# One more gate projection by seven products, and its gate written over a buffer that is already there

## The chip, the cores and the metric

The kernel runs on one core of one Trainium2 chip. The metric is the device time of one execution in microseconds (us). The kernel before takes 1662.96 us, the median of three runs that lie between 1662.33 and 1663.71 us.

A core has engines that run side by side, each with its own list of instructions in a fixed order. TensorE (PE in the profile, PEld for its weight loads) multiplies matrices. VectorE (DVE) and ScalarE (ACT) work elementwise. GpSimd (POOL) here issues most transfers and reduces a column over all partitions. SyncE (SP) issues the other transfers. On-chip memory (SBUF) has 128 partitions, and products accumulate in a second memory (PSUM).

## The reference

Two layers. Each normalises its input `h` (512 tokens of 2048 values), projects it, runs three groups of heads side by side, multiplies each by its own SiLU gate, and projects the result into the residual stream. What matters here is the short convolution, since the change lies in its gate, and the gated linear attention (GLA), whose work lies beside it:

```python
proj = h @ w_in
u = c_gate * h                                   # cv_c * cv_h
y = conv3(u) ; y_conv = cv_b * (y + bias) * silu(cv_g)
q, k, v, g = ...                                 # GLA: chunks of 64 tokens, state carried along
y_gla = rmsnorm(gla(q, k, v, g)) * silu(gl_g)
y_sb  = stick_breaking(...) * silu(sb_g)
out   = x + concat(y_conv, y_sb, y_gla) @ w_out
```

Each branch of the convolution (`h`, `b`, `c`, `g`) is 512 columns wide.

## The kernel before

**Weights.** All weight matrices are cut into groups of 256 columns (`specs`), taken one after the other. In each layer these are GLA's v 0, v 1, q, k, gate 0 and gate 1, then conv h 0, c 0, g 0 and b 0 (the first half of the convolution), then v, g, q and k for each of four pairs of attention heads, then conv h 1, c 1, g 1 and b 1, then eight groups of the output projection. A group of 2048x256 fp32 comes from DRAM into one of two buffers named `st`, as two transfers (`fetch`, L355, on POOL's queue). The transfer of group i+2 is issued when the computation of group i begins, and it has to wait until the last instruction has read the buffer that it goes to, so for the splits of group i (which shares the buffer).

**Splits.** Products are computed in fp16 with operands split into a high and a low part, three products for each. The scale of a group comes from squares of all its values (`wmax`, ACT at L367, twice, into an accumulator), a reduction over the partitions (POOL at L381) and four tiny instructions on DVE (L384 to L399). Then ACT writes the high part and DVE the low part. A plain group does so in two halves of 128x2048 (`whi` L436 and `wlo` L443). These steps of group i+1 hang on matmuls of group i (`hook`).

**Plain and quick groups.** A plain group of this kind is 96 matmuls of 128x512 (`project_cols`, L673 to L675). A group named in `QUICK_IN` is computed by seven products of half-size blocks in place of eight (`project_quick`, L765): 168 matmuls of 128x256. For this, `wsums` forms sums of the four weight blocks: one by an accumulating transfer within the buffer (L504, on POOL's queue), three by DVE (L507, L509, L512), and it splits seven parts of 128x1024 (ACT at L486, DVE at L487). The seven results are combined into the output by three copies on ACT (L780, L784, L787) and five instructions on DVE (L781, L788, L789, L791, L793). The blocks' sums for the input (`insums`) are made once in a layer. PSUM has three banks for projections.

**The convolution.** `conv_in(0)` projects h into `hb` (a buffer with the tag `qT`), then c, and multiplies the two into `uc` (L1167). After that nothing reads `hb`. `conv_out(0)` projects the gate with `project_gate`: for a plain group the gate is scaled out of PSUM into a buffer with the tag `g` (L842), and SiLU follows in steps (L844 to L848). Then it projects b, multiplies, and splits the result for the output projection with `mixsplit`, which uses the gate's buffer, dead by then, as its room.

**GLA.** It runs in two halves of two heads, interleaved with the groups on each engine. The decays of a chunk are made on DVE (L1038 to L1047) and ACT (L1002, L1011, L1040), put together on DVE (L1003, L1012), multiplied on PE (L1017, and then L1112), and closed by a norm (L1118 to L1130: PE averages at L1120, ACT and DVE finish).

**Order.** After a hand-ordered start, a scheduler in the compiler sets the fixed order of each engine, working with its own estimate of when each instruction could run. The code's `high_priority` blocks pull fetches, squares and splits ahead. A change in the code so moves other instructions too. The order of both kernels is known before they run; what it costs is not.

Of the kernel before, what the change touches and what calls it, by code (L numbers as in the profile page):

```python
# [17 lines left out]
P = 128  # L18
# [9 lines left out]


QUICK = ((3, 4, 6), (3, 4, 5, 6))  # L30
QUICK_IN = ("conv c 1", "gla gate 1", "conv g 1") + tuple(f"{n} {j}" for n in "gqk" for j in range(4))

AHEAD = (8, 17, 21)

# [9 lines left out]
def hybrid_trunk(ctx, tc, x, norm_g, w_in, conv_w, conv_b, sb_qn_g, sb_kn_g,  # L44
# [4 lines left out]
    seq = x.shape[1]  # L49
# [607 lines left out]
    for l in range(depth):  # L657
# [161 lines left out]
                ps.append(o)  # L819
                yield t, o, u  # L820

        def project_gate(mx=None, logistic=False):

            g = []

            def dst():
                g.append(wk([P, 2, seq], "g"))
                return g[0]

            ps, u = project(True, dst)  # L830
            quick_ = bool(g)
            g = dst() if not quick_ else g[0]
            for c in range(2):
                y = g[:, c, :]
                if logistic:
                    a = wk([P, seq], "ga") if quick_ else y
                    tables.append(S.activation(a, ps[c], AF.Sigmoid, scale=u))
                    for b in tables[-9:-1]:
                        order(tables[-1], b)
                    V.scalar_tensor_tensor(y, ps[c], u, a, ALU.mult, ALU.mult)  # L840
                    continue
                S.activation(y, ps[c], AF.Copy, scale=u)  # L842
                a = wk([P, seq], "ga")
                S.activation(a, y, AF.Abs)  # L844
                S.activation(a, a, AF.Exp, scale=-1.0)
                S.activation(a, a, AF.Ln, bias=1.0)
                V.scalar_tensor_tensor(a, y, 0.0, a, ALU.min, ALU.subtract)
                tables.append(S.activation(a, a, AF.Exp))  # L848
                V.tensor_tensor(y, y, a, ALU.mult)
            if mx is not None:  # L850
                V.tensor_reduce(mx, g, AX.XY, ALU.max, apply_absolute_value=True)
            return g, u
# [114 lines left out]
        for tag in ("qT", "kT"):  # L967
            o = wk([P, 2, seq], tag)
            ps, u = project(True, lambda: o)
# [187 lines left out]
        def conv_in(j, then=lambda: None):  # L1157

            hb = wk([P, 2, seq], "qT")
            ps, u = project(True, lambda: hb)  # L1160
            for c in range(2):
                S.activation(hb[:, c, :], ps[c], AF.Copy, scale=u)
            then()
            uc = wk([P, 2, seq], "raw", 1) if j else wk([P, 2, seq], "zw")
            ps, u = project(True, lambda: uc)
            for c in range(2):
                V.scalar_tensor_tensor(uc[:, c, :], ps[c], u, hb[:, c, :], ALU.mult, ALU.mult)  # L1167
            if j:
                mixload()
            y = wk([P, 2, seq], "kT")  # L1170
            for c in range(2):
                ch = 2 * j + c

                def w_(i):
                    return pcol("cw", (l * 3 + i) * 4 + ch)

                V.tensor_scalar(y[:, c, :], uc[:, c, :], w_(2), pcol("cb", l * 4 + ch), ALU.mult, ALU.add)
                for d in (1, 2):
                    V.scalar_tensor_tensor(y[:, c, d:], uc[:, c, :seq - d], w_(2 - d), y[:, c, d:], ALU.mult, ALU.add)
            then()  # L1180
            return y

        def conv_out(j, y, then=lambda: None):

            g, u = project_gate(logistic=j == 1)
            V.tensor_tensor(y, y, g, ALU.mult)
            bound = sm(2, "cm")

# [15 lines left out]
            for c in range(2):  # L1204
                mixsplit(2 * j + c, y[:, c, :], s_, g[:, c, :])

        conv_out(0, conv_in(0, lambda: norms.pop(0)()))


        later = []  # L1210
# [136 lines left out]
                go()  # L1347
            attend(j, *qkT, qz, vh, vl, vu, g, s_)

        conv_out(1, conv_in(1, go), go)  # L1350
        while later:
            go()
        if not last:
# [83 lines left out]
```

## Time and profile before

| | us |
|---|---|
| median of three runs | 1662.96 |
| the profiled execution: its time | 1662.23 |
| the profiled execution: span in the trace | 1660.4 |
| PE busy | 1636.1 (99%) |
| DVE busy | 1403.3 (85%) |
| ACT busy | 1181.9 (71%) |
| POOL busy | 258.6 (16%) |

The granted TensorE clock is 0.999 over the span. A row of a timeline gives the start of an instruction, its duration, engine, line, operation, what it writes and reads, the shapes and how many stand together; in brackets it tells how long the engine had been idle before it, and what released it. A matmul's duration contains its way through the array, and the next one starts before it ends: the distance of two starts is what one costs. In the table of windows each engine's busy time stands with its count of instructions in the order PE, PEld, DVE, ACT, POOL, then the granted clock, the share of the transfer engines and GB/s.

### The profile page before, as it was taken

What the parts mean: (1) busy time and instruction counts of PE and PEld (TensorE: products, weight loads), DVE (VectorE), ACT (ScalarE), POOL (GpSimd) and SP (SyncE); (2) the same over time, 40 slices, a digit from 0 to 9 for tenths busy, and PEclk for the clock granted to TensorE, in tenths of its full rate; (3) what the DMA queues carried; (4) which work ended last, traced back from release to release, by engine and by line L of the source; (5) the groups of instructions that cost most, each with busy time, mean ns of one, the idle gap of its engine ahead of it and who ended that gap; (6) DMA issues with size and microseconds to landing.
All of it is one profiled execution on the core that took longest, in us unless ns stands there. A gap on an engine that the chain in (4) does not pass through costs nothing. (4 is left out here: it accounts for less than half of the span.)

```text
span 1660.4 us, 39947 instructions
## 1 busy us (share of the span) xinstructions
PE 1636.1 (99%) x17098; PEld 1324.7 (80%) x17098; DVE 1403.3 (85%) x2323; ACT 1181.9 (71%) x1739; POOL 258.6 (16%) x298
## 2 busy tenths in 40 slices
PE   7999999999999999999999999999999999999999
PEld 5746548999998967799986465589898989668998
DVE  8978789979898979897599696998898989788893
ACT  8668787877777776755675786888686868666571
POOL 1121012111212121011111110112121212111110
PEclk9999999999999999999999999999999999999999
DMA  7144324576776868456433433436677676783441
GB/s 260 52 153 114 102 65 86 134 151 147 161 152 155 159 153 202 155 166 206 161 102 102 114 111 100 121 83 168 123 164 149 146 163 141 158 238 128 153 154 52
DMA packets 189747, 232.71 MB, mean 140 GB/s; under 512 B 90162, under 2 KB 149884, under 8 KB 189056
## 3 DMA queue, kind: packets, MB, share of 16 engines
q0 software_dynamic: 72832, 175.12, 38.9%
q1 hardware_dynamic: 107728, 45.56, 13.5%
q10 hardware_dynamic: 9008, 9.45, 1.7%
q8 instruction: 134, 2.20, 0.5%
q14 instruction: 45, 0.37, 0.1%
HBM read 179.65 MB, written 14.68 MB: 117 GB/s over the span
## 5 line engine op out<-in xcount | busy, mean ns | idle before, releaser
L486 ACT ACTIVATE wh<-st,ws 128x1024 f16<-128x1024 f32 x222 | 248.5, 1146 | 171.3 <-DVE st L507 68.1
L487 DVE SCALAR_TENSOR_TENSOR wl<-st,ws,wh 128x1024 f16<-128x1024 f32 x222 | 279.6, 1279 | 26.8 <-ACT wh L486 26.5
L367 ACT ACTIVATE junk<-st 128x2048 uint8<-128x2048 f32 x150 | 285.4, 1902 | 20.9 <-DMA st<-in_w_in_dram 13.9
L443 DVE SCALAR_TENSOR_TENSOR wl<-st,ws,wh 128x2048 f16<-128x2048 f32 x78 | 182.7, 2347 | 28.9 <-ACT wh L436 28.5
L685 PE MATMUL psp<-wl,m 128*128 128x256 f16 x704 | 191.9, 273 | 0.0
L684 PE MATMUL psp<-wh,m 128*128 128x256 f16 x704 | 191.9, 273 | 0.0
L686 PE MATMUL psp<-wh,m 128*128 128x256 f16 x704 | 191.9, 273 | 0.0
L436 ACT ACTIVATE wh<-st,ws 128x2048 f16<-128x2048 f32 x76 | 150.9, 1996 | 52.5 <-DVE ws L397 26.4
L768 PE MATMUL psp<-wh,s 128*128 128x128 f16 x2048 | 178.2, 219 | 3.9 <-DVE raw L788 3.7
L768 PEld LDWEIGHTS <-s 128*128 128x128 f16 x3072 | 173.2, 98 | 5.0 <-issue 4.7
L768 PE MATMUL psp<-wl,s 128*128 128x128 f16 x1024 | 172.8, 219 | 0.0
L381 POOL PARTITION_ALL_REDUCE wgm<-wm x75 | 43.1, 575 | 751.6 <-ACT junk L367 736.8
L355 POOL DMA_DIRECT2D st<-in_w_in_dram x114 | 101.8, 898 | 322.8 <-DVE wl L443 166.4
L765 PE MATMUL psp<-s,wh 128*128 128x256 f16 x896 | 151.9, 273 | 0.0
L765 PEld LDWEIGHTS <-wh 128*128 128x128 f16 x1344 | 131.4, 98 | 16.1 <-issue 1.0
L768 PEld LDWEIGHTS <-m 128*128 128x128 f16 x2160 | 122.7, 98 | 1.4 <-issue 1.0
L765 PE MATMUL psp<-s,wl 128*128 128x256 f16 x448 | 122.0, 273 | 0.0
L675 PEld LDWEIGHTS <-wl 128*128 128x128 f16 x576 | 56.3, 98 | 67.5 <-DVE wl L443 1.6
L675 PE MATMUL psp<-x,wl 128*128 128x512 f16 x288 | 109.0, 379 | 0.4 <-DVE wl L443 0.4
L674 PE MATMUL psp<-m,wh 128*128 128x512 f16 x288 | 109.2, 379 | 0.0
L674 PE MATMUL psp<-x,wh 128*128 128x512 f16 x288 | 109.2, 379 | 0.0
L675 PE MATMUL psp<-m,wl 128*128 128x512 f16 x288 | 109.0, 379 | 0.0
(422 smaller groups left out, 4147.8 us busy)
## 6 DMA issues: line engine op xcount, KB each, us to landing
st<-in_w_in_dram POOLq DMA_DIRECT2D x114, 1024.0 KB, 8.3
st<-in_w_out_dram POOLq DMA_DIRECT2D x32, 1024.0 KB, 8.4
st<-st POOLq DMA_DIRECT2D x30, 512.0 KB, 7.6
st<-in_w_in_dram SPq DMA_DIRECT2D x6, 1024.0 KB, 11.7
mixd<-g POOLq DMA_DIRECT2D x24, 256.0 KB, 5.7
x<-in_x_dram SPq DMA_DIRECT2D x4, 1024.0 KB, 4.8
qT<-in_x_dram ACTq DMA_DIRECT2D x8, 512.0 KB, 4.1
qT<-xs ACTq DMA_DIRECT2D x8, 512.0 KB, 3.9
```

The costliest lines, as they stand in the source:

```text
L367: sq = S.activation(junk(HK * GW).rearrange("p (k n) -> p k n", k=HK), staged[i][h], AF.Square, accum_out=peak[i][:, h:h + 1])
L436: hi = S.activation(wh[:, :, :GW], staged[i][h], AF.Copy, scale=scales[i])
L443: V.scalar_tensor_tensor(wl[:, :, :GW], staged[i][h], scales[i], wh[:, :, :GW], ALU.mult, ALU.subtract)
L486: hi = S.activation(h_, b, AF.Copy, scale=sc)
L487: V.scalar_tensor_tensor(l_, b, sc, h_, ALU.mult, ALU.subtract)
L674: T.matmul(o, wh[:, kk, cs], xl[:, :, k, :], start=False, stop=False)
L675: mm = T.matmul(o, wl[:, kk, cs], xh[:, :, k, :], start=False, stop=en)
L684: T.matmul(o, ah[:, t, k, :], wh[:, kk, :n], start=st_, stop=False, skip_group_check=True)
L685: T.matmul(o, ah[:, t, k, :], wl[:, kk, :n], start=False, stop=False, skip_group_check=True)
L686: return T.matmul(o, al[:, t, k, :], wh[:, kk, :n], start=False, stop=en, skip_group_check=True)
L765: mm = T.matmul(o, w[q_][:, kk, :], a[p_][:, :, kk, :], start=st_, stop=en, skip_group_check=True)
L768: mm = T.matmul(o[:, t * P:(t + 1) * P], a[p_][:, t, kk, :], w[q_][:, kk, :], start=st_, stop=en, skip_group_check=True)
```

## The change

The gate group of the convolution's first half, "conv g 0", joins the quick groups. As a quick group needs room for its result from its first products on, `project_gate` takes it as an argument: `conv_in` returns `hb` beside its result (in the first half of the convolution alone), and `conv_out` hands it to `project_gate`, which writes the gate there and takes no buffer with the tag `g`. `mixsplit` then uses that buffer as its room too. This holds in both layers.

```diff
-QUICK_IN = ("conv c 1", "gla gate 1", "conv g 1") + tuple(f"{n} {j}" for n in "gqk" for j in range(4))
+QUICK_IN = ("conv c 1", "gla gate 1", "conv g 1", "conv g 0") + tuple(f"{n} {j}" for n in "gqk" for j in range(4))
...
-        def project_gate(mx=None, logistic=False):
+        def project_gate(mx=None, logistic=False, room=None):
...
-                g.append(wk([P, 2, seq], "g"))
+                g.append(room or wk([P, 2, seq], "g"))
...
-            return y
+            return y, None if j else hb
 
-        def conv_out(j, y, then=lambda: None):
+        def conv_out(j, y, room, then=lambda: None):
 
-            g, u = project_gate(logistic=j == 1)
+            g, u = project_gate(logistic=j == 1, room=room)
...
-        conv_out(0, conv_in(0, lambda: norms.pop(0)()))
+        conv_out(0, *conv_in(0, lambda: norms.pop(0)()))
...
-        conv_out(1, conv_in(1, go), go)
+        conv_out(1, *conv_in(1, go), go)
```

The orders of the two kernels differ from conv c 0 up to about attention's second v group in each layer and are alike elsewhere. Three places of the first layer follow. The number behind a buffer's name tells its copies apart.

ACT, before, while PE computes conv g 0: the second closing norm of GLA's first half (`e_2042`, `e_2046`) with the squares of conv b 0's successor, v 0 (`junk_2811`, `junk_2813`); L1040 belongs to the second half of GLA:

```order
L1118 ACTIVATE e_2042<-psz_1976,gu_408 128x512
L877 ACTIVATE g_1461<-za_2036,gsmix_1485 128x512
L436 ACTIVATE wh_2707<-st_2511,ws_2699 128x8x256
L1122 ACTIVATE e_2046<-psm_2044,epst 128x512
L1123 ACTIVATE e_2046<-e_2046 128x512
L1124 ACTIVATE e_2042<-e_2046 128x512
L1126 ACTIVATE e_2042<-e_2042 128x512
L367 ACTIVATE junk_2811,wm_2810<-st_2660 128x2048
L1040 ACTIVATE e_2061<-e_2061 128x512
```

The same place after (v 0's squares are `junk_2908` and `junk_2910` here, the gate's buffer is `qT_2367`):

```order
L1118 ACTIVATE e_2042<-psz_1976,gu_408 128x512
L784 ACTIVATE qT_2367<-psp_2682 128x256
L877 ACTIVATE g_1461<-za_2036,gsmix_1485 128x512
L1122 ACTIVATE e_2046<-psm_2044,epst 128x512
L787 ACTIVATE qT_2367<-psp_2681 128x256
L1123 ACTIVATE e_2046<-e_2046 128x512
L367 ACTIVATE junk_2908,wm_2907<-st_2678 128x2048
L1124 ACTIVATE e_2042<-e_2046 128x512
L367 ACTIVATE junk_2910,wm_2907<-st_2678 128x2048
L842 ACTIVATE qT_2367<-qT_2367,wu_2552 128x512 x2
L1126 ACTIVATE e_2042<-e_2042 128x512
L436 ACTIVATE wh_2942<-st_2678,ws_2938 128x8x256
```

The two squares of v 0, two of the output copies of the gate and its scaling (L842) have come in between the norm's steps; the last step of the norm (L1126) stands behind them all.

DVE, before, at the same place, the end of the norm and the first instruction of GLA's second half (`e_2061`):

```order
L443 SCALAR_TENSOR_TENSOR wl_2708<-st_2511,ws_2699,wh_2707 128x8x256
L1125 SCALAR_TENSOR_TENSOR e_2042<-psm_2044,e_2042 128x512
L1127 TENSOR_TENSOR e_2046<-e_2046,e_2042 128x512
L1129 SCALAR_TENSOR_TENSOR za_2053<-psz_1976,gu_408,e_2046 128x512
L1038 TENSOR_TENSOR e_2061<-raw_941 128x256
L1039 TENSOR_TENSOR e_2061<-raw_941 128x256
```

And after, where `wq_2933` is the scale of v 0:

```order
L791 TENSOR_TENSOR qT_2367<-psp_2682,qT_2367 128x256
L793 TENSOR_TENSOR qT_2367<-psp_2682,qT_2367 128x256
L1125 SCALAR_TENSOR_TENSOR e_2042<-psm_2044,e_2042 128x512
L384 TENSOR_TENSOR wq_2933<-wgm_2934 128x1
L393 TENSOR_SCALAR wq_2933<-wq_2933 128x1
L397 TENSOR_SCALAR ws_2938<-wq_2933 128x1
L399 TENSOR_SCALAR wu_2940<-wq_2933,inoff_155 128x1
L1290 TENSOR_SCALAR vu_3280<-wu_2940 128x1
L1291 TENSOR_SCALAR vu_3280<-wu_2940 128x1
L1127 TENSOR_TENSOR e_2046<-e_2046,e_2042 128x512
L1129 SCALAR_TENSOR_TENSOR za_2053<-psz_1976,gu_408,e_2046 128x512
L1038 TENSOR_TENSOR e_2061<-raw_941 128x256
```

The last two output instructions of conv g 0 (L791, L793) and the scale of v 0 (L384 to L1291, which hang on v 0's squares) now stand ahead of the start of GLA's second half.

PE, before, in the middle of v 0 (`psp_2944`), at the last score products of GLA's second half (`psz_2298`, `psz_2308`), which need the decays that L1011 and L1012 put into `th_987`:

```order
L1017 MATMUL psz_2298<-th_987,qp_986 128x256
L1017 LDWEIGHTS qp_986
L1017 MATMUL psz_2298<-th_987,qp_986 128x512
L1017 LDWEIGHTS qp_986
L1017 MATMUL psz_2308<-th_987,qp_986 128x512
L684 LDWEIGHTS x_184
L684 MATMUL psp_2944<-wh_2849,x_184 128x256
```

After, these stand in attention's g 0, a group later: behind the first matmul of the fourth of its seven products (`psp_3288`) and ahead of the first that needs this product's low part (`wh_3107` and `wl_3108` hold the parts of the third and the fourth product):

```order
L765 LDWEIGHTS wh_3107
L765 MATMUL psp_3288<-s_1277,wh_3107 128x256
L1017 LDWEIGHTS qp_986
L1017 MATMUL psz_2298<-th_987,qp_986 128x256
L1017 LDWEIGHTS qp_986
L1017 MATMUL psz_2308<-th_987,qp_986 128x512
L765 LDWEIGHTS wl_3108
L765 MATMUL psp_3288<-s_1277,wl_3108 128x256
```

So the matmuls of GLA's second half have moved back on PE by about one group.

## The prediction

> **What bounds the kernel now.** I read the busy line first, then the waits of PE, then a table of windows around the changed group, then the timelines of DVE, ACT and POOL there.
>
> ```profile
> PE 1636.1 (99%) x17098; PEld 1324.7 (80%) x17098; DVE 1403.3 (85%) x2323; ACT 1181.9 (71%) x1739; POOL 258.6 (16%) x298
> ```
>
> ```profile
> PE psp L768 <- DVE raw L788: 3.7, 5, 0.7
> ...
> PE psp L765 <- DVE w7l L487: 1.8, 2, 0.9
> ...
> PE psz L1112 <- DVE za L1100: 0.4, 2, 0.2
> ```
>
> ```profile
> 208.40:230.00 21.60, 21.60 (x100) 9.79 (x99) 17.01 (x28) 15.45 (x18) 3.08 (x4) 1.00 0.29 87
> 230.00:253.40 23.40, 23.40 (x146) 12.06 (x145) 21.95 (x48) 20.84 (x37) 2.58 (x4) 1.00 0.20 63
> 253.40:279.60 26.20, 26.20 (x268) 23.25 (x267) 25.95 (x54) 18.66 (x39) 3.75 (x4) 1.00 0.43 95
> ```
>
> PE never stops for long: time goes down only if PE has less to do, and goes up if PE is made to wait. The windows are conv g 0, conv b 0 and a little more than v 0 of the first layer. PE is busy through all of each, at full clock. But the other engines are not idle beside it: DVE is busy 17.01 of 21.60 us while PE computes the changed group, then 21.95 of 23.40, then 25.95 of 26.20. DVE is nearly as full as PE right behind the change, because GLA's second half and the splits run there. The waits say that DVE's work there is in time now; the only wait of the region is L1112's, 0.2 us in each layer.
>
> **What PE saves.** The first and the last of four plain matmuls in a row, then three rows of seven-product ones:
>
> ```profile
> 211.00 0.38 PE L673 MATMUL psp<-x,wh 128*128 128x512 f16 x1
> ...
> 211.65 0.38 PE L673 MATMUL psp<-x,wh 128*128 128x512 f16 x1
> ...
> 300.08 0.27 PE L765 MATMUL psp<-x,w7l 128*128 128x256 f16 x1
> 300.19 0.38 PE L765 MATMUL psp<-x,w7h 128*128 128x256 f16 x2
> 300.40 0.27 PE L765 MATMUL psp<-x,w7l 128*128 128x256 f16 x1
> ```
>
> (211.65 - 211.00) / 3 is 0.216 us, and (300.40 - 300.08) / 3 is 0.109 (one row holds two). The group goes from 96 x 0.216 = 20.7 to 168 x 0.109 = 18.3 us, which saves 2.4 us a layer, 4.8 in all. Weight loads grow from 96 to 168; the row below gives 98 ns each, 16.5 us for all, which is under the 18.3 and stays covered.
>
> **What the splits and copies cost.** The kinds of instruction, each with its mean duration:
>
> ```profile
> L486 ACT ACTIVATE wh<-st,ws 128x1024 f16<-128x1024 f32 x222 | 248.5, 1146 | 171.3 <-DVE st L507 68.1
> L487 DVE SCALAR_TENSOR_TENSOR wl<-st,ws,wh 128x1024 f16<-128x1024 f32 x222 | 279.6, 1279 | 26.8 <-ACT wh L486 26.5
> L443 DVE SCALAR_TENSOR_TENSOR wl<-st,ws,wh 128x2048 f16<-128x2048 f32 x78 | 182.7, 2347 | 28.9 <-ACT wh L436 28.5
> L436 ACT ACTIVATE wh<-st,ws 128x2048 f16<-128x2048 f32 x76 | 150.9, 1996 | 52.5 <-DVE ws L397 26.4
> L765 PEld LDWEIGHTS <-wh 128*128 128x128 f16 x1344 | 131.4, 98 | 16.1 <-issue 1.0
> ...
> L507 DVE TENSOR_TENSOR st<-st 128x1024 f32<-128x1024 f32 x30 | 36.7, 1223 | 1.8 <-DMA st<-st 1.1
> L781 DVE TENSOR_TENSOR g<-psp,g 128x256 f32<-128x256 f32 x19 | 7.9, 418 | 3.5 <-ACT g L780 3.5
> ```
>
> DVE gets seven L487, three sums like L507 and five output steps like L781, and loses two L443: 7 x 1.28 + 3 x 1.22 + 5 x 0.42 - 2 x 2.35 = +10.0 us a layer. ACT gets seven L486 and three copies (about 0.4 each, since DVE's of the same size take that) and loses two L436: 7 x 1.15 + 1.2 - 4.0 = +5.2 us. POOL gets one transfer of 512 KB within SBUF. None of that is PE's work. The group's own splits lie beside conv h 0 and c 0, early enough, and the last, needed by the seventh product at 208.4 + 6 x 2.61 = 224.1, is made at about 217. What counts is who stands behind them.
>
> ```profile
> 198.69 1.79 POOL L355 DMA_DIRECT2D st<-in_w_in_dram  x2 [10.24 <-DVE wl L443]
> ...
> st<-in_w_in_dram POOLq DMA_DIRECT2D x114, 1024.0 KB, 8.3
> ```
>
> v 0's weights go into the buffer that conv g 0 leaves. Before, the fetch is issued at 198.69, released by the second plain split. After, it waits for the last of seven splits, about 217.2 by my walk along DVE's new order with the durations above. At 8.3 us to landing the two halves are there at about 225.5 and 227.
>
> **The stall that I expect.** The buffer written over costs no time: `hb` is last read by L1167 at 208.62, and the first copy into it comes after conv g 0's first product. The gate's scaling reads SBUF in place of PSUM, at the same size. The order is what costs.
>
> ```profile
> 224.44 0.69 DVE L1127 TENSOR_TENSOR e<-e,e 128x512 f32<-128x512 f32 x1 [0.70 <-ACT e L1126]
> 225.17 0.75 DVE L1129 SCALAR_TENSOR_TENSOR za<-psz,gu,e 128x512 f32<-128x512 f32 x1
> 225.84 0.41 DVE L1038 TENSOR_TENSOR e<-raw 128x256 f32<-128x256 f32 x1
> ...
> 228.49 1.89 ACT L367 ACTIVATE junk<-st 128x2048 uint8<-128x2048 f32 x1
> 230.29 0.19 ACT L367 ACTIVATION_READ_ACCUMULATOR junk<-st 128x1 f32 x1
> ...
> 230.65 0.40 POOL L381 PARTITION_ALL_REDUCE wgm<-wm  x1 [0.25 <-ACT junk L367]
> ```
>
> GLA's second half starts on DVE with L1038, at 225.84. After, DVE's order puts the scale of v 0 ahead of it, and ACT's order puts both squares of v 0, the copy L787 and two L842 ahead of the norm's last step L1126. The first square starts when its half has landed, at about 225.7; each takes 1.89 and about 0.1 for the accumulator, and L1124 between them 0.5, so both are done at 230.2. POOL's 0.40 brings DVE's scale to about 231, its five tiny instructions to 231.9; two L842 and L1126 end about there as well; L1127 and L1129 follow, 0.7 each, and L1038 starts at about 233.4, 7.6 us late.
>
> ```profile
> 225.84:260.74 34.90, 33.27 (x72) 1.00 0.49 138
> ...
> 216.59 0.74 DVE L878 SCALAR_TENSOR_TENSOR g<-za,gsmix,g 128x512 f16<-128x512 f32 x1
> L1062 DVE SCALAR_TENSOR_TENSOR qp<-e,qp 128x512 f16<-128x512 f32 x4 | 2.9, 722 | 0.0
> L1052 DVE COPY_PREDICATED zw<-masks,psz 128x512 f32<-128x512 uint8 x28 | 24.8, 886 | 3.2 <-PE psz L1017 3.1
> ```
>
> From there to the last L1012 DVE takes 34.90 us in before, busy 33.27 of them (72 instructions). In the new order this stretch holds two L487, two L878, an L507, an L1062 and an L1052 more, which have come back from behind: 2.56 + 1.48 + 1.22 + 0.72 + 0.89 = 6.9, less 0.08 for each overlap with the next (starts stand 0.33 apart at a duration of 0.41), so 6.3. With the old idle time filled it is 39.6, with it kept 41.2: the last L1012 ends at 273.0 to 274.6, where it ended at 260.74.
>
> ```profile
> 260.77 0.40 ACT L1082 ACTIVATE e<-raw,nT 128x128 f32<-128x128 f32 x1
> ...
> 264.16 1.14 ACT L486 ACTIVATE wh<-st,ws 128x1024 f16<-128x1024 f32 x1
> 265.20 0.84 ACT L1011 ACTIVATE th<-e 64x256 f16<-64x256 f32 x2
> ...
> 266.44 1.32 ACT L877 ACTIVATE g<-kT,csmix 128x512 f16<-128x512 f32 x2
> 267.67 0.84 ACT L1011 ACTIVATE th<-e 64x256 f16<-64x256 f32 x2
> ```
>
> ACT then goes from L1082 to the last L1011 in 268.51 - 260.77 = 7.7 us. In the new order three more L486 (1.04 each by the starts above) and two squares (1.89) stand in that stretch, and the two L877 (1.23) have gone: 3.1 + 3.8 - 1.2 = +5.7, so 13.4. The last decay is ready at 286.4 to 288.0.
>
> PE comes to the matmul that needs it after conv g 0 (18.3), conv b 0 (20.7), v 0 (192 matmuls of 128x256, 20.9), 73 matmuls of attention's g 0 (8.0), and GLA's matmuls and averages between, mostly 84 of 128x128:
>
> ```profile
> 237.60 0.61 PE L1017 MATMUL psz<-th,qp 128*128 128x128 f16 x8
> ```
>
> (0.61 less one duration of 0.22, over 7, is 0.056, so 4.7; the averages add 0.7.) 208.4 + 73.3 = 281.7. PE waits 4.7 to 6.3 us; I take 5.5, the middle, as nothing tells whether the old idle time is filled. Behind it the old wait at L1112 (0.2) goes. A layer gives 5.5 - 2.4 - 0.2 = +2.9 us. The second layer has the same order and the same work:
>
> ```profile
> 1025.40 0.75 DVE L1167 SCALAR_TENSOR_TENSOR zw<-psp,wu,qT 128x512 f32<-128x512 f32 x1 [5.34 <-PE psp L675]
> 1070.00:1096.00 26.00, 25.75 (x54) 1.00 0.43 96
> ```
>
> It stands 816.8 us later with the same 5.34 us of idle time ahead, and DVE is as full. Twice 2.9 is +5.8: 1662.2 (the profiled execution) becomes 1668.0. That execution lies 0.7 us under the median of the runs, so against the median it is 1668.7.
>
> The Trainium skill ("Perfetto Trace Analysis", Tensor Engine Instruction) states that ACT, DVE and GpSimd take their instructions strictly first in, first out, and that only PE can pull weight loads ahead. By that rule L1038, whose own input is long there, stands behind the scale of v 0 and the 7.6 us are late in full; were it otherwise, the first rival would hold. The row of L1127 agrees: DVE idles 0.70 us ahead of it, with L1038 ready behind.
>
> **The rivals.**
>
> The cover holds (faster). If DVE and ACT finish by 281.7, PE saves 2.4 and the 0.2 at L1112 in each layer: 1662.96 - 5.2 = 1657.8. For it: ACT has idle time in these windows (6.15 of 21.60), so my walk may be too slow by some waits that overlap. Against: DVE had 1.7 us left in the last two windows together, and it gets more. It decides if L1038 starts late by under about 2.1 us (7.6 less the stall of 5.5, the rest of the walk unchanged).
>
> The squares of v 0 don't hold DVE up, and only the gate's last step L793 does (about the same). L793 waits for PE's last product, at 208.4 + 18.3 + 0.4 = 227.1, and the norm's two steps follow after L1126, so L1038 starts at about 229.9. Everything is 3.5 us earlier, the stall is 1.2 to 2.8, and a layer gives -1.4 to +0.2: 1660.2 to 1663.4. For it: the fetch may land sooner than the median. Against: the order itself puts the scale ahead.
>
> The fetch of v 0 lands later (slower still). It shares the engines with the accumulating transfer, which takes up to 10.7 us to landing in before where its median is 7.6:
>
> ```profile
> DMA to landing us min/median/max: 6.4/7.6/10.7
> ```
>
> If the fetch loses the same 3.1 us, the stall grows by 3.1 a layer: 1674.9.
>
> **How the numbers follow.** A change within 0.2% (3.3 us) is about what a measurement of this kernel cannot tell from none. The stall as walked has 0.50, the late fetch 0.10, the second rival 0.18, the first 0.22. The likeliest gives 1668.7, and alone 1667.2 to 1670.4 by its bounds. Of the stall's 0.50 I leave 0.03 to a stall so much smaller that it counts as the same. So slower is 0.57, same 0.21, faster 0.22. The range reaches from 1658.5, which cuts off most of the first rival's lower side, to 1674.
>
> **What would show it.** Right: conv g 0 takes 18.3 us on PE; L1038 of GLA's second half starts 7 to 8 us later than 225.84; a new wait of PE of about 5 us at L1017 or at the fourth product of attention's g 0, near 282 in the first layer and near 1099 in the second; v 0's fetch issued near 217. Wrong: no wait of PE over 1 us there (then the first rival), or a wait elsewhere, for example ahead of v 0's first matmuls because its splits come late, or in attention's later groups, where I found DVE and ACT in time again.

## The result, and the profile after

The changed kernel takes 1677.4 us, the median of five runs (1673.99 to 1684.71); the kernel before, in the runs beside it, 1663.71 us (1662.33 to 1665.94). The ratio is 1.0066 with a 95% interval of 1.0039 to 1.0093: slower, by 6.5 to 15.5 us. The forecast was slower, by 5.7 us; the median lies 3.4 us above the range. The profiled execution took 1680.55 us, its span is 1678.7, the granted clock 0.994.

The busy line of after, then its waits of PE (what PE wanted to write, what it waited for; us in total, times, the longest):

```profile
PE 1639.6 (98%) x17242; PEld 1342.7 (80%) x17242; DVE 1421.0 (85%) x2349; ACT 1189.5 (71%) x1755; POOL 263.8 (16%) x300
```

```profile
PE psz L1228 <- DMA kT<-qp: 6.1, 2, 5.8
...
PE psz L1017 <- ACT th L1011: 2.5, 4, 1.1
PE psp L684 <- ACT m L1152: 2.2, 1, 2.2
PE psp L765 <- DVE wl L487: 2.1, 2, 1.1
```

The expected wait is there, at L1017 and, by L487, at the fourth product: 2.5 + 2.1 us over both layers, where 11 were forecast. The longest wait is one that the prediction doesn't have: L1228, the scores of attention's first pair, waits for a transpose. (L684's wait for L1152 is at the first layer's output projection; it is taken up with the experiments.)

To see where the time came from I set the starts of the projection groups of both traces side by side. The rows below are the first matmuls of v 1 in the first layer and of g 1 (the g group of the second pair of heads, right behind the first pair's scores) in the second, in after:

```profile
341.61 0.27 PE L684 MATMUL psp<-wh,x 128*128 128x256 f16 x1
...
1194.55 0.42 PE L765 MATMUL psp<-m,wh 128*128 128x256 f16 x1
```

| a group's first matmul | before | after | after is later by |
|---|---|---|---|
| first layer, conv b 0 | 229.99 | 227.61 | -2.4 |
| first layer, attention's v 1 | 340.18 | 341.61 | +1.4 |
| first layer, k 1 | 403.26 | 407.87 | +4.6 |
| first layer, second half of conv b 1 | 665.55 | 669.33 | +3.8 |
| first layer, second half of the output projection's first group | 685.05 | 692.94 | +7.9 |
| second layer, conv g 0 | 1025.19 | 1032.14 | +7.0 |
| second layer, v 1 | 1156.94 | 1163.97 | +7.0 |
| second layer, attention's g 1 | 1179.53 | 1194.55 | +15.0 |
| second layer, second half of g 1 | 1184.77 | 1200.66 | +15.9 |
| last group | 1651.39 | 1669.69 | +18.3 |

In the second layer the stretch from conv g 0 to v 1, which holds the saving and the forecast stall, costs 0.1 us. The loss stands behind it: 3.2 us right behind v 1 in the first layer, 8.9 in the second, 4.1 at the output projection, and 2.4 in small pieces to the end, which I did not take apart; 0.8 and 0.9 come back ahead of and behind the output projection. (The two profiled executions lie 18.3 us apart, the medians 13.7.) The 3.2 us of the first layer are not at L1228, both of whose waits are in the second. PE waits there behind the first pair's scores: 0.34 us for L486, and 1.59 and 0.65 for L781, an output step on DVE. None of the three is in the trace of before. The longest:

```profile
378.86 0.27 PE L765 MATMUL psp<-x,wh 128*128 128x256 f16 x1 [1.59 <-DVE g L781]
```

### The profile page after: what moved, and what is told of

Read it like the earlier page. It is cut to its first block, busy times and chain, and to the rows that moved or that the text cites. A ratio compares the mean times of both kernels' runs of the same rounds, so it can differ in the third digit from the quotient of the medians.

```text
span 1678.7 us, 40271 instructions
## 1 busy us (share of the span) xinstructions
PE 1639.6 (98%) x17242; PEld 1342.7 (80%) x17242; DVE 1421.0 (85%) x2349; ACT 1189.5 (71%) x1755; POOL 263.8 (16%) x300
## 3 DMA queue, kind: packets, MB, share of 16 engines
q1 hardware_dynamic: 107728, 45.56, 13.7%
## 4 chain that ended last, share of the span: by engine, by line
PE 56%; DVE 22%; DMA 9%; ACT 7%; issue 4%; POOL 0%; DVEq 0%; ACTq 0%; SPq 0%; POOLq 0%
PE psp L768 12%; PE psp L765 6%; PE psp L815 5%; PE psp L674 5%; PE psp L675 5%; PE psp L673 5%; PE psp L684 4%; PE psp L686 4%; PE psp L685 4%; DVE wl L487 4%; DMA st<-in_w_in_dram 4%; ACT junk L367 3%; DVE za L1244 2%; DMA qT<-qp 2%; DMA th<-za 2%
## 5 line engine op out<-in xcount | busy, mean ns | idle before, releaser
L486 ACT ACTIVATE wh<-st,ws 128x1024 f16<-128x1024 f32 x234 | 261.7, 1146 | 158.3 <-DVE st L507 67.6
L487 DVE SCALAR_TENSOR_TENSOR wl<-st,ws,wh 128x1024 f16<-128x1024 f32 x234 | 295.0, 1280 | 31.5 <-ACT wh L486 31.4
L684 PE MATMUL psp<-wh,m 128*128 128x256 f16 x704 | 192.6, 274 | 2.2 <-ACT m L1152 2.2
L443 DVE SCALAR_TENSOR_TENSOR wl<-st,ws,wh 128x2048 f16<-128x2048 f32 x74 | 173.2, 2348 | 16.6 <-ACT wh L436 16.2
L765 PE MATMUL psp<-s,wh 128*128 128x256 f16 x1024 | 174.3, 274 | 0.0
L765 PEld LDWEIGHTS <-wh 128*128 128x128 f16 x1536 | 151.0, 98 | 20.1 <-issue 1.6
L765 PE MATMUL psp<-s,wl 128*128 128x256 f16 x512 | 139.8, 274 | 2.1 <-DVE wl L487 2.1
L675 PE MATMUL psp<-x,wl 128*128 128x512 f16 x256 | 97.0, 379 | 0.4 <-DVE wl L443 0.4
L675 PE MATMUL psp<-m,wl 128*128 128x512 f16 x256 | 97.0, 379 | 0.0
L674 PE MATMUL psp<-x,wh 128*128 128x512 f16 x256 | 97.0, 379 | 0.0
L674 PE MATMUL psp<-m,wh 128*128 128x512 f16 x256 | 97.0, 379 | 0.0
```

Source lines behind the costliest of these rows:

```text
L443: V.scalar_tensor_tensor(wl[:, :, :GW], staged[i][h], scales[i], wh[:, :, :GW], ALU.mult, ALU.subtract)
L486: hi = S.activation(h_, b, AF.Copy, scale=sc)
L487: V.scalar_tensor_tensor(l_, b, sc, h_, ALU.mult, ALU.subtract)
L674: T.matmul(o, wh[:, kk, cs], xl[:, :, k, :], start=False, stop=False)
L675: mm = T.matmul(o, wl[:, kk, cs], xh[:, :, k, :], start=False, stop=en)
L684: T.matmul(o, ah[:, t, k, :], wh[:, kk, :n], start=st_, stop=False, skip_group_check=True)
```

## Experiments

Each ratio is to runs of the kernel before on the same chip. The expectations name theories by letters: A is the order-bound loss of the prediction, B chance in one execution, C blames the buffer that the gate is written over, D the buffer in which k's split waits for q's transposes, E those transposes themselves, F the exchange of two instructions ahead of them, G transfers that collide whatever their order.

### The loss again, and whether the room, the seven products or the order makes it

**The changed kernel again.**

> The changed kernel once more, unaltered, for a second trace. Theory A (the loss is fixed by the order: GLA's second half starts on DVE 7.9 us later, PE waits about 2.8 us a layer there, and the backlog on DVE and ACT reaches the first attention pair): the waits of PE at L1017, and at the fourth product of attention's g 0, come back within 0.3 us in both layers, DVE's L1038 starts again near 233.7, and the time is 1674 to 1680. Theory B (most of the loss is chance of that one execution, transfers that collided and a halved TensorE clock behind a wait): the GLA waits come back, but the 5.8 us at L1228 of the second layer and the wait at L684 behind ACT's L1152 do not both come back, and the time is 1666 to 1672.

1676.95 us, ratio 1.0081 (1.0058 to 1.0105). In this trace L1017 waits 2.2 us and L765 for L487 2.1, as in after. The other two are:

```profile
PE psp L684 <- ACT m L1152: 9.7, 1, 9.7
PE psz L1228 <- DMA kT<-qp: 6.7, 2, 6.4
```

L1228's wait comes back, so the loss is not chance of one execution (B falls); L1152's varies: 2.2 us in after, 9.7 here.

**The gate in a buffer of its own**, as before, the seven products kept:

```diff
-                g.append(room or wk([P, 2, seq], "g"))
+                g.append(wk([P, 2, seq], "g"))
```

> conv g 0 by seven products as in the changed kernel, but its gate goes into a buffer of its own with the tag g, and not over the h values. Theory A (seven products and the order that comes with them cost the time, the room nothing): like the changed kernel, 1668 to 1680. Theory C (the buffer qT, which now lives until the convolution's split has left it, holds up the attention's q transposes, which take the same tag): faster than before by 3 to 5 us, 1658 to 1661, since the saving on PE stays and the hold-up goes.

1696.23 us, 1.0171 (1.0123 to 1.0218), which neither theory had. Without the room the loss more than doubles: the scheduler then makes another order, in which the stall of the prediction is really large. So this run doesn't test the room alone; C falls further down, where the room stays and the loss goes.

```profile
PE psz L1017 <- ACT th L1011: 19.1, 6, 6.7
```

**The room alone**, "conv g 0" plain again:

```diff
-QUICK_IN = ("conv c 1", "gla gate 1", "conv g 1", "conv g 0") + tuple(f"{n} {j}" for n in "gqk" for j in range(4))
+QUICK_IN = ("conv c 1", "gla gate 1", "conv g 1") + tuple(f"{n} {j}" for n in "gqk" for j in range(4))
```

> The gate written over the h values, but conv g 0 computed as 96 plain matmuls as before. Theory A: as before, 1661 to 1666. Theory C: slower than before by more than 3 us, with a later start of the transposes into qT in the first attention pair.

1667.32 us, 1.0022 (1.0001 to 1.0043). Writing the gate over `hb` in a plain group costs some 0.2%, at the edge of what the interval tells from none; most of the loss comes with the seven products.

**GLA's second half first.** v 0's squares are held back behind the norm's last step on ACT (L1126), so that DVE's L1038 need not wait for v 0's scale (`closing` is a dictionary that this and later edits add; `order(a, b)` puts a behind b):

```diff
-                    order(a, mm)
+                    order(a, mm), order(a, closing.get(i, mm))
...
-                S.activation(sq, sq, AF.Copy, scale=-0.5, bias=1.5)
+                closing[38 * l + 10 if hh and not p else -1] = S.activation(sq, sq, AF.Copy, scale=-0.5, bias=1.5)
```

> The changed kernel, with ACT's squares of attention's v 0 put behind the last step (L1126) of the closing norm of GLA's first half, in both layers; nothing else is touched by hand. Theory A: DVE's L1038 starts about 2 us earlier than 233.7, near 231.5, PE's waits in GLA's second half fall from 2.8 to about 1 us a layer, and the time falls to 1664 to 1672. If v 0's squares do not hold GLA up, L1038 stays near 233.7 and the time near the changed kernel's.

1681.99 us, 1.0091 (1.0063 to 1.0119). L1038 does start earlier (229.83 in place of 233.71), and the wait at L1017 is gone, but another has come, and L1228's is still there:

```profile
PE psp L765 <- ACT wh L486: 5.7, 2, 2.9
PE psz L1228 <- DMA kT<-qp: 5.4, 2, 4.5
```

The expectation was missed: what the prediction took for the cause can be taken away without the loss going away.

### The buffer of q's parts, and one layer at a time

q's and k's split parts share one buffer (`qp`), so k's split on ACT (L1340) waits until q's two transposes (L1345) have read it. **k's parts in another buffer** take that wait away:

```diff
-                parts = wk([P, 2, NT * GW], "qp", 1, F16)
+                parts = wk([P, 2, NT * GW], "raw" if n else "qp", 1, F16)
```

> The changed kernel, but the split of attention's k goes into the buffer raw (free by then) and not into qp, which q's transposes still read; the order on every engine is the same as the changed kernel's. Theory D (what the loss in the second layer hangs on is k's split waiting for q's transposes, which now meet a weight fetch): ACT's L1340 for k starts 7 to 12 us earlier, near 350 and 1173, PE's wait at L1228 in the second layer falls from about 6 us to under 2 (q's own transposes still have to land), the TensorE clock stays at full speed there, and the time falls by 6 to 9 us against the changed kernel, to 1667 to 1671. Rival E (the transfer engines are full there, and k's transposes only queue behind q's): L1340 starts earlier, but the wait at L1228 stays above 3 us and the time within 3 us of the changed kernel's.

1678.23 us, 1.0064 (1.0034 to 1.0093), so the median is no better. ACT no longer waits for q's transposes, and PE still waits for k's:

```profile
352.83 1.06 ACT L1340 ACTIVATE raw<-kT 128x1024 f16<-128x1024 f32 x1 [4.32 <-DVE kT L1336]
```

```profile
PE psz L1228 <- DMA kT<-raw: 4.3, 2, 2.2
```

As the whole cause the buffer (D) falls; the transposes themselves come late (E). The buffer has a part in it: in this trace the stretch behind v 1 costs 0.1 us in the first layer and 6.1 in the second, where after has 3.2 and 8.9. The runs spread from 1668.94 to 1697.38 us, so the median does not show so much.

**The same edit on the kernel before.**

> The same edit in the kernel before, again with the same order on every engine. Theories D and E: no PE wait hangs on it there (k's split waits 0.6 to 0.7 us for DVE, not for the transposes), so the time is that of the kernel before within 0.2%.

1666.25 us, 0.9999 (0.9986 to 1.0013): it costs and brings nothing there. Its trace has a wait of PE for L1152 of 6.4 us, which the trace of before lacks. So this wait also comes to a kernel without the change; the 4.1 us at the output projection in the table above (2.2 us of wait, and a lower clock behind it) are no proof of a cause in the change.

**The change in the first layer alone, and in the second alone:**

```diff
-        if name in (QUICK[l] if src is w_out else QUICK_IN):
+        if name in (QUICK[l] if src is w_out else QUICK_IN) and (name, l) != ("conv g 0", 1):
...
-            return y, None if j else hb
+            return y, None if j or l == 1 else hb
```

(with 0 in place of 1 for the second layer alone).

> The change in the first layer alone; the order of the second layer is that of the kernel before. Theory A with D: a small loss, 1 to 6 us (GLA waits of 2.5 against a saving of 2.4, and waits of 1 to 4 behind it in attention), 1665 to 1670. If the two layers lose alike, it is half of the loss of the changed kernel, 6 to 7 us.

> The change in the second layer alone; the order of the first layer is that of the kernel before. Theory A with D: most of the loss, 7 to 11 us, with the wait of about 6 us at L1228 behind k's transposes again, 1671 to 1675. If the L1228 wait in the second layer needs the delays that the first layer adds, it is gone and the time is within 4 us of the kernel before.

First layer alone: 1678.14 us, 1.0052 (1.0028 to 1.0077). Second alone: 1671.12 us, 1.0045 (1.0017 to 1.0074). I had expected most of the loss in the second, and the medians don't show it. The trace of the first has a wait of 15.0 us at L1152, that of the second (its fastest run, 1664.48 us) almost nothing at L1228, so neither explains its own median. The runs of the first fall into two groups, five from 1664.6 to 1670.1 us and seven from 1677.8 to 1686.8. Its trace, the slowest run, loses 3.0 us behind v 1 and 19.7 at the output projection; without the latter it would lie in the lower group. So the exchange taken up next, with 3.0 us in this trace, does not account for that median; whether the wait at L1152 does stays open. In the second, q's transposes hold ACT up for 7.71 us:

```profile
1173.23 1.06 ACT L1340 ACTIVATE qp<-kT 128x1024 f16<-128x1024 f32 x1 [7.71 <-DMA qT<-qp]
```

### The exchange at attention's first pair

DVE's order of both kernels ahead of the first pair's q differs by one exchange, in both layers (before, then after; the first layer's rows, L443 makes the low parts of v 1's weights out of `st`, L1341 those of q):

```
L443 SCALAR_TENSOR_TENSOR wl_3954<-st_3426,ws_3949,wh_3953 128x8x256
L1341 SCALAR_TENSOR_TENSOR qp_3831<-raw_3425,qp_3831 128x1024
L443 SCALAR_TENSOR_TENSOR wl_3958<-st_3426,ws_3949,wh_3957 128x8x256

L443 SCALAR_TENSOR_TENSOR wl_4051<-st_3523,ws_4046,wh_4050 128x8x256
L443 SCALAR_TENSOR_TENSOR wl_4055<-st_3523,ws_4046,wh_4054 128x8x256
L1341 SCALAR_TENSOR_TENSOR qp_3928<-raw_3522,qp_3928 128x1024
```

The second L443 is the last reader of `st`, so it releases the next fetch; L1341 makes what q's second transpose reads. The timelines of before (rows of several engines, the others left out) show the transpose issued first and the fetch 2.5 us behind it:

```profile
334.70 1.22 DVE L1341 SCALAR_TENSOR_TENSOR qp<-raw,qp 128x1024 f16<-128x1024 f32 x1
335.84 2.35 DVE L443 SCALAR_TENSOR_TENSOR wl<-st,ws,wh 128x2048 f16<-128x2048 f32 x1
335.95 3.08 SPq L1345 DMA_TRANSPOSE qT<-qp  x1
...
338.48 1.75 POOL L355 DMA_DIRECT2D st<-in_w_in_dram  x2 [6.49 <-DVE wl L443]
...
347.74 1.06 ACT L1340 ACTIVATE qp<-kT 128x1024 f16<-128x1024 f32 x1 [0.70 <-DVE kT L1336]
```

Those of after, both layers, show the fetch ahead of the transpose:

```profile
342.14 1.23 DVE L1341 SCALAR_TENSOR_TENSOR qp<-raw,qp 128x1024 f16<-128x1024 f32 x1
342.52 1.76 POOL L355 DMA_DIRECT2D st<-in_w_in_dram  x2 [3.87 <-DVE wl L443]
343.39 1.81 SPq L1345 DMA_TRANSPOSE qT<-qp  x1
357.48 1.06 ACT L1340 ACTIVATE qp<-kT 128x1024 f16<-128x1024 f32 x1 [8.02 <-DMA qT<-qp]
...
1164.88 1.77 POOL L355 DMA_DIRECT2D st<-in_w_in_dram  x2 [3.87 <-DVE wl L443]
1165.75 6.01 SPq L1345 DMA_TRANSPOSE qT<-qp  x1
1185.80 1.06 ACT L1340 ACTIVATE qp<-kT 128x1024 f16<-128x1024 f32 x1 [12.82 <-DMA qT<-qp]
1190.93 0.59 PE L1228 MATMUL psz<-kT,qT 128*128 128x512 f16 x1 [5.84 <-DMA kT<-qp]
```

From the issue of q's second transpose to the split of k that it releases go 14.1 us in the first layer (357.48 - 343.39) and 20.0 in the second; before it was at most 11.8, and ACT then waited for DVE, not for the transpose. k's own transposes follow as much later, and PE waits for them 5.84 us. Theory F: this exchange, with q already late, is the loss.

**The exchange undone in the changed kernel**, nothing else:

```diff
-        V.scalar_tensor_tensor(wl[:, :, :GW], staged[i][h], scales[i], wh[:, :, :GW], ALU.mult, ALU.subtract)
+        lo = V.scalar_tensor_tensor(wl[:, :, :GW], staged[i][h], scales[i], wh[:, :, :GW], ALU.mult, ALU.subtract); h and i in closing and order(lo, closing[i])
...
-                V.scalar_tensor_tensor(parts[:, 1], raw.rearrange("p t c -> p (t c)"), top, parts[:, 0],
+                closing[38 * l + 14 if j + n == 0 else -1] = V.scalar_tensor_tensor(parts[:, 1], raw.rearrange("p t c -> p (t c)"), top, parts[:, 0],
```

> The changed kernel with two neighbours on DVE swapped in each layer: the low part of attention's first q (L1341) stands again ahead of the second low-part split of v 1 (L443), as in the kernel before; nothing else in the order differs. Theory F (that swap is what sets the loss behind GLA: L443 frees the buffer for the next weight fetch, so in the changed kernel the fetch is issued before q's second transpose and the two share the transfer engines): q's second transpose is issued about 2.3 us ahead of the fetch, ACT's L1340 for k waits under 2 us for it (8 and 13 in the changed kernel), PE's wait of about 6 us at L1228 in the second layer is gone, and the time falls by 6 to 10 us, to 1664 to 1669. Rival G (the transfers collide wherever they come that late, whatever their order): the waits stay, and the time stays within 3 us of the changed kernel's.

1665.91 us, 0.9998 (0.9974 to 1.0022). The whole loss is gone, though the room stays (so C falls) and q still comes late (so G falls): ACT's first split of it stands at 337.84, against 332.30 in before. The timeline, first layer and then second:

```profile
338.92 1.22 DVE L1341 SCALAR_TENSOR_TENSOR qp<-raw,qp 128x1024 f16<-128x1024 f32 x1 [0.30 <-ACT qp L1340]
340.06 2.34 DVE L443 SCALAR_TENSOR_TENSOR wl<-st,ws,wh 128x2048 f16<-128x2048 f32 x1
...
352.58 1.06 ACT L1340 ACTIVATE qp<-kT 128x1024 f16<-128x1024 f32 x1 [4.32 <-DVE kT L1336]
...
1179.77 1.06 ACT L1340 ACTIVATE qp<-kT 128x1024 f16<-128x1024 f32 x1 [4.32 <-DVE kT L1336]
```

ACT waits for DVE again, as before the change, and PE has no wait at L1228, nor the three behind it in the first layer: from v 1 to k 1 there, and from v 1 to the second half of g 1 in the second layer, PE takes as long as in before. PE's waits at L1017 and for L487 are about as in after (2.2 us each over both layers): this loss and the forecast one are separate.

**The exchange alone, put into the kernel before** (the same lines, with `order(closing[i], lo)`).

> The kernel before with the opposite swap in each layer: v 1's second L443 ahead of q's L1341, nothing else. Theory F: ACT's L1340 for k, which waits 0.6 to 0.7 us for DVE before, waits 4 to 8 us for q's transposes, PE waits at L1228 in one layer or both, and the time rises by 2 to 8 us. Rival G: no change beyond 0.2%.

1665.14 us, 0.9991 (0.9975 to 1.0007):

```profile
337.90 1.76 POOL L355 DMA_DIRECT2D st<-in_w_in_dram  x2 [5.93 <-DVE wl L443]
338.77 1.23 SPq L1345 DMA_TRANSPOSE qT<-qp  x1
...
350.27 1.06 ACT L1340 ACTIVATE qp<-kT 128x1024 f16<-128x1024 f32 x1 [3.92 <-DMA qT<-qp]
```

The fetch stands ahead of the transpose here too, and the split of k comes 11.5 us after the transpose's issue and waits 3.92 us for it; but PE does not wait at L1228, and the time doesn't change. F had a rise of 2 to 8 us here and was missed: the exchange costs nothing by itself. It costs in the changed kernel, where q already comes late: ACT's first split of q stands at 332.30 in before and at 339.19 in after, 6.9 us later, with PE only 1.4 us later. Each of the two alone, q late without the exchange (0.9998) and the exchange with q in time (0.9991), costs nothing that these runs can tell. That the lateness, and nothing else in which the two orders differ, is the other condition fits this, but no run has set it alone.

**A shorter way through the norm.** High parts of weight splits are ordered behind each norm's L1126 on ACT, so that L1038 starts earlier, without (chain) and with (chain_q) the exchange undone:

```diff
-        hi = S.activation(wh[:, :, :GW], staged[i][h], AF.Copy, scale=scales[i])
+        hi = S.activation(wh[:, :, :GW], staged[i][h], AF.Copy, scale=scales[i]); (i, 0) in closing and order(hi, closing[i, 0])
...
-            hi = S.activation(h_, b, AF.Copy, scale=sc)
+            hi = S.activation(h_, b, AF.Copy, scale=sc); n > 2 and (i, 0) in closing and order(hi, closing[i, 0])
...
-                S.activation(sq, sq, AF.Copy, scale=-0.5, bias=1.5)
+                closing[-1 if p else (38 * l + 8 + hh, 0)] = S.activation(sq, sq, AF.Copy, scale=-0.5, bias=1.5)
```

> The changed kernel with the closing norms of GLA's first half kept together on ACT: the late splits of conv g 0 stand behind the first norm's last step, and the splits of conv b 0 behind the second's. The swap of L443 and L1341 is as in the changed kernel. Theory A (GLA's waits come from the late start of its second half on DVE): L1038 starts between 219 and 224 in place of 233.7, the waits of PE at L1017 and at the fourth product of attention's g 0 (2.5 us a layer) go, and the time falls by 5 us against the changed kernel if the waits in attention stay, to 1668 to 1672.

> Both edits: the norms kept together, and L1341 ahead of the second L443. Theories A and F together: no wait of PE over 1 us between 181 and 400 us or at its counterpart in the second layer, the saving of 2.4 us a layer is left, and the time is 1657 to 1662, faster than the kernel before by 2 to 5 us. If something else eats the gain, it is within 0.2% of the kernel before or slower.

Without: 1679.59 us, 1.0093 (1.0059 to 1.0126). With: 1670.77 us, 1.0028 (1.0012 to 1.0045). L1038 starts at 225.42, ahead of before's 225.84 (less far than I had expected), and the wait at L1017 for ACT is gone, but plain splits are late instead. Both expectations of the time were missed, by 7.6 and 8.8 us. The waits without the exchange undone:

```profile
PE psz L1228 <- DMA kT<-qp: 5.8, 2, 5.0
PE psp L675 <- DVE wl L443: 4.1, 3, 1.8
```

The exchange makes 8.8 us between the two medians, and with it undone L1228 does not wait: the same finding on another order.

### Whether ACT limits GLA's second half

With the exchange undone, the squares of attention's q 0 are put behind the last decay on ACT (L1011):

```diff
-                    order(a, mm)
+                    order(a, mm), order(a, closing.get((i, 1), mm))
...
-                S.activation(hi, eh, AF.Copy)
+                closing[38 * l + 12, 1] = S.activation(hi, eh, AF.Copy)
```

> The changed kernel with L1341 ahead of v 1's second L443, as in the run q_first, and with ACT's two squares of attention's q 0 put behind the last decay (L1011) of GLA's second half, in both layers. If the waits of PE in GLA's second half (2.5 us a layer, at L1017 and at the fourth product of attention's g 0) are what cancels the saving of 2.4 us a layer, they fall to under 1 us a layer, since 3.8 us of ACT's work leave the stretch ahead of them, and the time is 1658 to 1663, 2 to 5 us under the run q_first and the kernel before. If the late squares make the splits of q 0 late in turn, PE waits there instead, and the time is that of the kernel before or above it.

1668.3 us, 1.0024 (1.0000 to 1.0048):

```profile
PE psp L765 <- DVE wl L487: 2.8, 2, 1.4
...
PE psz L1017 <- DVE th L1012: 1.8, 2, 0.9
```

The same matmul now waits for DVE in place of ACT, nearly as long. A window of after, from L1038 to the last decay, agrees: DVE is busy 49.85 of 50.29 us, with 98 instructions.

```profile
233.71:284.00 50.29, 49.01 (x427) 37.59 (x426) 49.85 (x98) 40.43 (x73) 8.66 (x9) 1.00 0.31 71
```

DVE is full there, and ordering ACT anew brought nothing. No version that I ran is faster than the kernel before by more than its interval.

## Why the prediction was right and wrong

**What PE saves: right.** conv b 0 starts 2.4 us earlier.

**The fetch, the scale and the late start of GLA's second half: right.** Forecast were 217.2, about 231 and 233.4:

```profile
217.79 1.81 POOL L355 DMA_DIRECT2D st<-in_w_in_dram  x2 [8.40 <-DVE w7l L487]
...
231.14 0.16 DVE L384 TENSOR_TENSOR wq<-wgm 128x1 f32<-128x1 f32 x1 [1.77 <-POOL wgm L381]
...
233.71 0.41 DVE L1038 TENSOR_TENSOR e<-raw 128x256 f32<-128x256 f32 x1
```

The sentence of the Trainium skill ("Perfetto Trace Analysis", Tensor Engine Instruction: strict order on DVE) agrees with that: L1038 did stand behind v 0's scale.

**The stall: right in place, mis-sized.** The term was 5.5 us a layer. The rows of the first layer, ACT's stretch and then PE:

```profile
270.90 0.40 ACT L1082 ACTIVATE e<-raw,nT 128x128 f32<-128x128 f32 x1 [0.32 <-DVE qp L1062]
...
283.25 0.84 ACT L1011 ACTIVATE th<-e 64x256 f16<-64x256 f32 x2
```

```profile
282.75 0.27 PE L1017 MATMUL psz<-th,qp 128*128 128x256 f16 x1 [0.15 <-ACT th L1011]
...
284.13 0.38 PE L1017 MATMUL psz<-th,qp 128*128 128x512 f16 x1 [1.12 <-ACT th L1011]
...
285.58 0.39 PE L765 MATMUL psp<-s,wl 128*128 128x256 f16 x1 [1.08 <-DVE wl L487]
```

0.15 + 1.12 + 1.08 is 2.35 us. The last L1012 ended at 274.0 (273.58 and 0.42), inside the forecast 273.0 to 274.6, and ACT's stretch is 284.09 - 270.90 = 13.2 us long, where 13.4 were forecast. But I had let the stretch begin behind the last L1012; its first L1082 hang on L1062, and it began at 270.90, some 3 us earlier. So the stall of a layer is about as large as the saving: the net of that part is 0.1 us in the second layer and 1.4 in the first, in place of 2.9. By this step alone the kernel would be the same, and with the exchange undone it is (0.9998).

**Attention's later groups: the step that failed.** "Or in attention's later groups, where I found DVE and ACT in time again" is where the loss is. I followed the two engines to the end of GLA's second half and took what lies behind to be as before, at no cost; the text on the change has the orders differ up to about attention's second v group. The exchange of L1341 and L443 stands right there, and I did not ask which transfer each of the two releases. It became a loss in a kernel in which q is 6.9 us late, behind the full DVE that I had worked out. The trace of after puts 8.9 us to it in the second layer and 3.2 in the first, 12.1 of the 13.7 us between the medians; undoing it gives back the whole 0.66% to 0.81%.

**The rivals.** The first (the cover holds, 1657.8) had PE's saving right, but the stall was there. The second (L1038 at 229.9) did not come. The third (v 0's fetch lands later still) did not either: the scale stood at 231.14, as for a fetch in time. The sign was right by luck: the part that the forecast rests on, saving and stall, nets 1.5 us over both layers in place of 5.8, and the loss came from a place that was taken as free.

## What to carry to other kernels

Where a scheduler moves instructions, look in the new order for an exchange of an instruction that frees a buffer with one that makes the input of another transfer: it changes which transfer is issued first, and here that was worth more than the microseconds of the two instructions. The saving on the engine that is the bound was given back here where a second engine was already nearly full beside it, so ask of each stretch behind the change how much that engine has left. And follow lateness past the first place where it costs, to the next transfer that hangs on it.

## What the runs showed of the hardware that was not expected

**A fetch, an accumulating transfer and transposes in flight together.** These are the transfers of the second layer's stretch, in after (1162 to 1186 us) and with the exchange undone (1164 to 1180): KB each, and the median from issue to landing.

```profile
st<-in_w_in_dram POOLq DMA_DIRECT2D x2, 1024.0 KB, 16.3
st<-st POOLq DMA_DIRECT2D x1, 512.0 KB, 17.0
```

```profile
st<-in_w_in_dram POOLq DMA_DIRECT2D x2, 1024.0 KB, 9.7
st<-st POOLq DMA_DIRECT2D x1, 512.0 KB, 9.7
```

And a window of six microseconds behind the transposes' issue, in after and with the exchange undone; the last two columns are the share of the transfer engines and GB/s:

```profile
1168.00:1174.00 6.00, 6.00 (x57) 5.39 (x55) 2.48 (x10) 4.79 (x15) 1.99 (x2) 1.00 1.22 62
```

```profile
1169.00:1175.00 6.00, 6.00 (x57) 5.37 (x56) 2.00 (x9) 5.28 (x17) 3.57 (x4) 1.00 1.20 257
```

By the trace the transfer engines are as busy in both, and move a quarter as much in after. Over the whole trace the accumulating transfer (L504) takes from 6.4 to 10.7 us to landing in before; its row in after (with the exchange undone only the longest differs, 10.8):

```profile
DMA to landing us min/median/max: 6.4/7.6/17.0
```

The medians are the same; the 17.0 us are this one place, and the next longest in after is 11.5. It comes back: the transfer takes 16.8, 16.7 and 17.5 us here in the traces of after_again, gla_first and chain, and 9.7 and 10.8 with the exchange undone (q_first, chain_q). Why the packets take so long in that order is not settled, nor why the second layer is hit harder: with the change in the second layer alone, ACT's wait for the transposes was 7.71 us and not 12.82.

**The wait at L1152**, at the output projection, is between none and 15.0 us over the traces, also in a kernel without the change. It adds to the spread of single runs of both kernels (the kernel before lay between 1660.75 and 1687.66 us over all its runs). A single trace's table of where time went must be read against that. It goes back to transfers too. L1152 stands on ACT behind L912, and in the trace of the change in the first layer alone that instruction waits 20.78 us for a load (`ga`), which SP issues behind three loads of the output projection's input (L888):

```profile
700.04 0.42 ACT L912 ACTIVATE za<-ga 16x256 bf16<-16x256 f32 x1 [20.78 <-DMA ga<-in_gla_w_up_dram]
```

L888 takes up to 27.6 us to landing there, where before has 13.8, and the two halves of the weight fetch (1 MB each) issued a few microseconds ahead take 22.9 in the median, where before has 9.8. Transposes (L1252) are issued just ahead of that fetch, in both traces, so it may be the same thing as at attention's first pair; that is not shown. Of the ten traces with the seven products in the first layer five have a wait at L1152 of over 1 us, of the five without them one: too few to say whether the change makes it more frequent.

**The granted clock halves behind short waits, but not each time.** In after the three waits of PE are the same in both layers to 0.02 us (0.15, 1.12, 1.08 and 0.15, 1.12, 1.06). The windows behind them, first layer and second:

```profile
284.00:290.00 6.00, 4.79 (x30) 3.39 (x29) 5.88 (x12) 3.30 (x8) 0.00 (x0) 0.72 0.69 78
1107.70:1113.70 6.00, 4.78 (x37) 3.49 (x37) 5.88 (x12) 3.73 (x9) 0.00 (x0) 1.00 0.71 80
```

The mean clock is 0.72 in the one and 1.00 in the other; with the exchange undone it is the other way round, 1.00 in the first layer and 0.72 in the second, and the stretch up to v 1 then costs 0.1 us in the first layer and 1.8 in the second, counted as in the table. Single microseconds in the slow window are at 0.50, and it is worth the 1.3 us by which the first layer's stretch is dearer than the second's. The Trainium skill ("TensorE: Matmul & The Clock Gate", Part 1: The HAM clock gate) says that the gate is at half or full rate and looks at a free-running window of about 3.4 us. The traces agree: the rate is halved, and equal waits fare differently, as they would by where the window falls. They differ in that no wait here is as long as an idle window; matmuls stand between the three.
